# Gate products of the last 128 tokens: float32 against two float32r parts, in a four-layer decoder trunk on one core

## The chip, the core and the metric

The kernel runs on one core of a Trainium2 chip. The metric is the time of one execution on the device in microseconds; several executions are taken and their median is given. One further execution is recorded by the hardware profiler; all rows below come from that one.

Engine names: PE is the matrix engine (PEld its weight loads), DVE the vector engine, ACT the scalar engine, POOL the general one, SP the engine that issues most transfers.

## The reference, cut to what matters

A decoder trunk of four layers works on 256 tokens of 1024 values. Each layer has a token mixer and then `peer`, an expert layer. The change lies in `peer`:

```
def peer(x, w_q, keys, u, v):
    ...
    best, sel = lax.top_k(cand.reshape(n_tok, PEER_HEADS, PEER_TOPK * PEER_TOPK), PEER_TOPK)
    idx = jnp.take_along_axis(cand_idx.reshape(n_tok, PEER_HEADS, -1), sel, axis=-1)
    gate = jax.nn.softmax(best, axis=-1)
    ...
        h = jax.nn.gelu(jnp.einsum('cd,ced->ce', tc, ue).astype(f32), approximate=False)
        return jnp.einsum('ce,ced->cd', gc * h, ve)
```

Each token chooses 8 heads x 16 experts out of 16384, with a softmax gate for each. The kernel does not gather experts. It computes the hidden value of all 16384 experts for all tokens, multiplies it by a dense table of gates that is zero where an expert was not chosen, and multiplies the outcome by all of `v`.

## The kernel before, in words

The work of a layer is written as one stream of 128x1024 weight chunks. `_load` (line 81) has SP fetch a chunk, `_split` (lines 91 and 97) has ACT round it to a float32r high part and DVE subtract that for the low part. `nxt` hands out a chunk and first splits those up to two chunks ahead. A product of float32 quality is then three float32r products: high by high, low by high, high by low (`proj_t`, line 141; `proj_n`, lines 151 to 155).

`peer` has four steps. `peer_scores` makes the routing scores. The first big loop (j from 0 to 127) multiplies chunk j of `u` by the tokens (24 products of 256 columns into a bank `hp`), and ACT writes the Gelu of it to G (line 1051). The second big loop multiplies G, split into parts (lines 1036 and 1037), by the chunks of `v`. Beside the first loop runs the routing: `topk_gen` on DVE, 128 tokens at a time.

The gates get to G in two ways. For the first 128 tokens POOL scatters them into a table in DRAM (`scatter`, line 957), 128 indirect transfers; at j = 124 SP is told to fetch the table piece by piece (`fetch`, line 1022), which waits for the whole scatter, and DVE multiplies G by the pieces (line 1031). For the last 128 tokens `weights_gen` makes the gates on PE, four tokens a unit, 32 units a layer: for each token the product of two one-hot tables, one of the row and one of the column of each chosen expert, the second multiplied by the gate. `topk_gen` ends by transposing row, column and gate into `tab` (line 911).

`weights_gen` is a generator. Each `yield` is a turn, and `pace` gives turns out as the first loop goes on: after the routing is done the rate is 35 turns over the chunks that are left up to 125. In turn u the code before does this:

- `build(u + 1)`: DVE makes both one-hot tables of the next unit by comparing `iota` with `tab` (line 925) and multiplies the column's by the gates (line 927), into a buffer `wk` of two.
- PE: four products (line 941) into the bank `y{u % 4}`.
- `due()`: DVE multiplies the already activated chunks of G by the gates of the unit of two turns ago (line 1006, two pieces).
- `keep` for the last turn's unit: ACT stores its gates where G has not been activated yet (line 999), and a new `due` is kept for the rest.

Chunks that are activated after their gates were stored are taken care of by lines 1054 and 1013: ACT writes the Gelu to a buffer `gtmp` (two of them) and DVE multiplies it into G, one chunk later.

Every engine works in the order in which the code is written: the program is built with a manual schedule for PE, DVE, ACT and SP, and the framework adds the waits between them.

Of the kernel before, what the change touches and what calls it, by code (L numbers as in the profile page):

```python
# [11 lines left out]
F32 = mybir.dt.float32  # L12
F32R = mybir.dt.float32r
# [3 lines left out]
AF = mybir.ActivationFunctionType  # L17
# [27 lines left out]
class Kernel:  # L45
# [744 lines left out]
    def topk_gen(self, ids, val, tab, ready):  # L790


        nc = self.nc
        V = nc.vector
        svs, sis = self.ring(2, 16, 16), self.ring(2, 16, 16, dt=U32)
# [23 lines left out]
        for t in range(2):  # L819
# [9 lines left out]
            f = sif.rearrange("p (h q) k -> p h q k", q=2)  # L829
# [11 lines left out]
            for a, off in enumerate(OFFS):  # L841
                if a in (0, 1, 2, 3, 4, 5, 8):
                    nb = 16 // (a + 1)
                    na = len([1 for c in range(a, 16) if 16 // (c + 1) == nb])
                    o = cand[:, :, off:off + na * nb].rearrange("p h (a b) -> p h a b", b=nb)
# [7 lines left out]
            shape = [128, 4, 16, 16]  # L853
# [54 lines left out]
        p = self.small((128, 4, 128))  # L908
        for q in range(3):
            nc.tensor.transpose(p[:, q, :], stk[:, q, :], self.ident)  # L910
        V.tensor_copy(tab, p[:, 0:3, :])
        yield 0.55

    def weights_gen(self, tab, keep):


        nc = self.nc
        V = nc.vector
        shape = [128, 2, 4, 128]
        units = {}  # L920

        def build(u):
            ts = slice(124 - 4 * u, 128 - 4 * u)
            ab = self.misc.tile(shape, F32, name="wk", bufs=2)
            V.tensor_tensor(ab, self.iota[:, None, None, :].to_broadcast(shape),  # L925
                            tab[:, 0:2, ts][:, :, :, None].to_broadcast(shape), op=OP.is_equal)
            V.tensor_mul(ab[:, 1], ab[:, 1], tab[:, 2, ts][:, :, None].to_broadcast([128, 4, 128]))
            units[u] = ab

        build(0)  # L930
        yield 1
        kept, due = None, None
        for u in range(34):
            if u + 1 < 32:
                build(u + 1)
            p = None
            if u < 32:
                p = self.ps.tile([128, 4, 128], F32, name=f"y{u % 4}", bufs=1)
                ab = units.pop(u)
                for k in range(4):  # L940
                    nc.tensor.matmul(p[:, k, :], ab[:, 0, k, :], ab[:, 1, k, :], start=True, stop=True)  # L941
            if due is not None:
                due()
            due = keep(256 - 4 * u, kept.rearrange("p t j -> p j t")) if kept is not None else None
            kept = p
            yield 1

# [25 lines left out]
    def peer(self, i, turn):  # L973
        nc = self.nc
        self.new_work()
        iv = self.misc.tile([128, 2, 128], F32, name="gt", bufs=2)
        ids, val = iv[:, 0, :].bitcast(I32), iv[:, 1, :]
        tab = self.misc.tile([128, 3, 128], F32, name="tab", bufs=1)
        self.sc = self.carve(2, 16, 128)
        self.sc_ready, self.paced = 0, 0.0  # L980
        sent = []
# [11 lines left out]
        def keep(t0, p):  # L993

            ts = slice(t0, t0 + 4)
            n = [min(max(done[0] - 64 * f, 0), 64) for f in range(2)]
            for f in range(2):
                if n[f] < 64:
                    nc.scalar.activation(G[f][:, n[f]:64, ts], p[:, 64 * f + n[f]:64 * f + 64, :], AF.Copy)
            done[1] = t0  # L1000

            def due():
                for f in range(2):
                    if n[f]:
                        g = G[f][:, 0:n[f], ts]
                        nc.vector.tensor_mul(g, g, p[:, 64 * f:64 * f + n[f], :])
            return due
# [32 lines left out]
        for j in range(128):  # L1040
# [11 lines left out]
            if td < T:  # L1052
                tmp = self.misc.tile([128, T], F32, name="gtmp", bufs=2)
# [27 lines left out]
        for j in range(n):  # L1081
# [12 lines left out]
            if j in (68, 71, 74, 77):  # L1094
                k = (j - 68) // 3
                self.load_norms(i, nc.sync, slice(k, k + 1))
            if j in (80, 83, 86, 89):
                k = (j - 80) // 3
# [234 lines left out]
```

## Time and profile before

| | before |
|---|---|
| median of 3 runs | 3824.62 us (3823.56 to 3825.99) |
| the profiled execution, its own time | 3826.61 us |
| its span from first to last instruction | 3824.8 us |
| PE busy | 3792.5 us, 99% |
| DVE busy | 2826.6 us, 74% |
| ACT busy | 1878.3 us, 49% |
| POOL busy | 1091.9 us, 29% |

Busy time counts an engine's instructions and not its waits. In the lists of groups a row gives the line, engine, operation, names and shape, the count, then busy time in us and the mean ns of one, then the idle time of the engine just before them and what ended it. In a timeline a row gives the start, the length, the engine, the line and what it was, with the idle time before it in brackets. An arrow points to what a thing was made from or what ended a wait.

### The profile page before, as it was taken

How to read it: one execution, taken by the hardware profiler on the slowest of the kernel's cores; microseconds unless marked ns; L12 is line 12 of the kernel's file. 1: busy time of each engine (PE TensorE's matmuls, PEld its weight loads, DVE VectorE, ACT ScalarE, POOL GpSimd, SP SyncE). 2: the span in 40 equal slices, each digit the busy share in tenths (PEclk: the TensorE clock that was granted, in tenths of full speed). 3: DMA queues.
4: the chain of work that ended last, by engine and by line, in shares of the span. 5: the costliest groups of instructions: out<-in, count | busy, mean ns of one | idle time of the engine just before them, and what ended most of it. 6: DMA issues, size and time to landing. Idle time of an engine off the chain costs nothing. (4 is left out here: it accounts for less than half of the span.)

```text
span 3824.8 us, 67261 instructions
## 1 busy us (share of the span) xinstructions
PE 3792.5 (99%) x25652; PEld 3468.1 (91%) x25652; DVE 2826.6 (74%) x5914; ACT 1878.3 (49%) x3400; POOL 1091.9 (29%) x548
## 2 busy tenths in 40 slices
PE   8999999999999999999999999999999999999999
PEld 7999998888998999988887999998888899998887
DVE  7787776676667887766667788776677788776666
ACT  5544444545554544455555444444555554445554
POOL 0158750000000188720000148860000128780000
PEclk9999999999999999999999999999999999999999
DMA  7667777775444577777762567778775456666665
GB/s 236 201 183 180 174 207 239 246 242 163 142 138 147 171 186 178 176 226 240 250 211 99 168 182 180 177 185 246 245 249 164 144 182 179 160 158 215 215 226 176
DMA packets 400996, 735.35 MB, mean 192 GB/s; under 512 B 102608, under 2 KB 240400, under 8 KB 400160
## 3 DMA queue, kind: packets, MB, share of 16 engines
q1 hardware_dynamic: 326688, 730.60, 59.4%
q0 software_dynamic: 73792, 0.38, 5.5%
q8 instruction: 201, 3.29, 0.3%
q14 instruction: 123, 1.01, 0.1%
q10 hardware_dynamic: 192, 0.07, 0.0%
HBM read 696.01 MB, written 34.89 MB: 191 GB/s over the span
## 5 line engine op out<-in xcount | busy, mean ns | idle before, releaser
L97 DVE TENSOR_TENSOR lo<-raw,hi 128x1024 fp32r<-128x1024 f32 x1182 | 1444.2, 1223 | 595.2 <-ACT hi L91 591.9
L91 ACT ACTIVATE hi<-raw 128x1024 fp32r<-128x1024 f32 x1212 | 1271.2, 1050 | 32.9 <-DMA raw<-in_peer_v 21.2
L957 POOL DMA_INDIRECT gates<-gt x512 | 1017.6, 1988 | 485.0 <-DVE G L808 247.7
L141 PE MATMUL hp<-zh,hi 128*128 128x256 f32 x5312 | 764.0, 286 | 1.6 <-ACT zh L242 0.7
L141 PE MATMUL hp<-zh,lo 128*128 128x256 f32 x5312 | 746.4, 283 | 0.0
L141 PE MATMUL hp<-zl,hi 128*128 128x256 f32 x5312 | 746.1, 283 | 0.0
L141 PEld LDWEIGHTS hp<-zh,hi 128*128 128x128 f32 x5312 | 682.7, 192 | 7.6 <-issue 4.5
L141 PEld LDWEIGHTS hp<-zh,lo 128*128 128x128 f32 x5312 | 685.9, 192 | 0.0
L141 PEld LDWEIGHTS hp<-zl,hi 128*128 128x128 f32 x5312 | 685.8, 192 | 0.0
L155 PE MATMUL y<-hi,wk 128*128 128x512 f32 x2004 | 624.9, 393 | 1.5 <-DVE wk L1037 1.3
L153 PE MATMUL y<-lo,wk 128*128 128x512 f32 x2004 | 623.1, 392 | 0.0
L151 PE MATMUL y<-hi,wk 128*128 128x512 f32 x2004 | 621.1, 390 | 0.0
L97 POOL TENSOR_TENSOR lo<-raw,hi 128x1024 fp32r<-128x1024 f32 x30 | 72.7, 2424 | 1871.8 <-ACT hi L91 1871.8
L1051 ACT ACTIVATE G<-hp 128x256 f32<-128x256 f32 (+26 forms) x512 | 182.6, 357 | 836.8 <-PE hp L141 825.9
L1036 ACT ACTIVATE wk<-G 128x256 fp32r<-128x256 f32 x492 | 205.9, 418 | 656.9 <-issue 625.1
L155 PEld LDWEIGHTS y<-hi,wk 128*128 128x128 f32 x2004 | 375.9, 188 | 85.5 <-DVE wk L1037 2.1
L151 PEld LDWEIGHTS y<-hi,wk 128*128 128x128 f32 x2004 | 375.8, 188 | 84.2 <-ACT wk L1113 0.3
L153 PEld LDWEIGHTS y<-lo,wk 128*128 128x128 f32 x2004 | 376.5, 188 | 80.1
L1037 DVE TENSOR_TENSOR wk<-G,wk 128x256 fp32r<-128x256 f32 x492 | 208.8, 424 | 263.3 <-ACT wk L1036 263.2
L427 ACT ACTIVATE G<-hp 128x256 f32<-128x256 f32 x156 | 59.7, 382 | 203.4 <-PE hp L141 195.9
L925 DVE TENSOR_TENSOR wk<-iota,tab 128x1024 f32<-128x1024 f32 x128 | 156.1, 1219 | 0.0
L1031 DVE TENSOR_TENSOR G<-G,gt 128x128 f32<-128x128 f32 x512 | 144.3, 284 | 7.6 <-DMA gt<-gates 7.4
(202 smaller groups left out, 2611.7 us busy)
## 6 DMA issues: line engine op xcount, KB each, us to landing
raw<-in_peer_u SPq DMA_DIRECT2D x512, 512.0 KB
raw<-in_peer_v SPq DMA_DIRECT2D x512, 512.0 KB
raw<-in_dil_w SPq DMA_DIRECT2D x72, 512.0 KB
gates<-zero SPq DMA_DIRECT2D x256, 128.0 KB
raw<-in_peer_wq SPq DMA_DIRECT2D x64, 512.0 KB
gt<-gates SPq DMA_DIRECT2D x256, 128.0 KB
raw<-in_swa_w SPq DMA_DIRECT2D x20, 512.0 KB
G<-in_lnp SPq DMA_DIRECT2D x16, 512.0 KB
```

The source lines that it names most:

```text
L91: nc.scalar.activation(h[:, :w], r[:, :w], AF.Copy)
L97: eng.tensor_sub(lo[:, :w], r[:, :w], h.bitcast(F32)[:, :w])
L141: mm(ps, w[:, k, :], z[:, k0 + k, :], start=(p == 0 and k == 0), stop=(p == 2 and k == nk - 1))
L151: mm(ps[t][b][:, :s.stop - s.start], zh[:, ts], hi[:, s], start=first, stop=False)
L153: mm(ps[t][b][:, :s.stop - s.start], zh[:, ts], lo[:, s], start=False, stop=False)
L155: mm(ps[t][b][:, :s.stop - s.start], zl[:, ts], hi[:, s], start=False, stop=last)
L925: V.tensor_tensor(ab, self.iota[:, None, None, :].to_broadcast(shape), tab[:, 0:2, ts][:, :, :, None].to_broadcast(shape), op=OP.is_equal)
L957: ins = self.nc.gpsimd.indirect_dma_start(self.gates[i], IndirectOffsetOnAxis(ap=ids[:, k:k + 1], axis=0), val[:, k:k + 1], None, compute_ ...
L1031: nc.vector.tensor_mul(g, g, gts[j // 2][:, j % 2, :])
L1036: nc.scalar.activation(gz[:, 0, :], g, AF.Copy)
L1037: nc.vector.tensor_sub(gz[:, 1, :], g, gz.bitcast(F32)[:, 0, :])
L1051: nc.scalar.activation(g[:, 0:td], ps[:, 0:td], AF.Gelu)
```

## The change

The gate products become float32r. `topk_gen` splits the gates in `tab` into a float32r part and the rest. `build` makes the one-hots in float32r; ACT multiplies the column's one-hots by the rest, token by token, into a third table, and DVE then multiplies them in place by the first part. One product of 256 columns per token gives both halves, with two tokens to a bank, so that a unit takes two banks (`y0` and `y1`, or `y2` and `y3`). `add` sums the halves: ACT copies the second to `gtmp` and DVE adds it to the first, bank by bank, both into the first bank. `due()` stands at the head of the turn, ahead of `build`.

```
-        V.tensor_copy(tab, p[:, 0:3, :])
+        V.tensor_copy(tab[:, 0:3], p[:, 0:3, :])
         yield 0.55
+        V.tensor_copy(tab[:, 3].bitcast(F32R), tab[:, 2])
+        yield 0.28
+        V.tensor_sub(tab[:, 2], tab[:, 2], tab[:, 3])
+        yield 0.28
...
         def build(u):
-            ts = slice(124 - 4 * u, 128 - 4 * u)
-            ab = self.misc.tile(shape, F32, name="wk", bufs=2)
-            V.tensor_tensor(ab, self.iota[:, None, None, :].to_broadcast(shape),
+            o = 124 - 4 * u
+            ts = slice(o, o + 4)
+            ab = self.misc.tile([128, 3, 4, 128], F32R, name="wk", bufs=2)
+            ones = ab.bitcast(F32)[:, 1]
+            V.tensor_tensor(ab[:, 0:2], self.iota[:, None, None, :].to_broadcast(shape),
                             tab[:, 0:2, ts][:, :, :, None].to_broadcast(shape), op=OP.is_equal)
-            V.tensor_mul(ab[:, 1], ab[:, 1], tab[:, 2, ts][:, :, None].to_broadcast([128, 4, 128]))
+            for k in range(4):
+                nc.scalar.activation(ab[:, 2, k, :], ones[:, k, :], AF.Copy, scale=tab[:, 2, o + k:o + k + 1])
+            V.tensor_mul(ab[:, 1], ones, tab[:, 3, ts][:, :, None].to_broadcast([128, 4, 128]))
             units[u] = ab
+
+        def add(p):
+
+            for q in range(2):
+                tmp = self.misc.tile([128, 2, 128], F32, name="gtmp", bufs=2)
+                nc.scalar.activation(tmp, p[q][:, :, 1, :], AF.Copy)
+                V.tensor_add(p[0][:, :, q, :], p[q][:, :, 0, :], tmp)
+            return p[0].rearrange("p a b j -> p (a b) j")
...
         for u in range(34):
+            if due is not None:
+                due()
             if u + 1 < 32:
                 build(u + 1)
             p = None
             if u < 32:
-                p = self.ps.tile([128, 4, 128], F32, name=f"y{u % 4}", bufs=1)
+                p = [self.ps.tile([128, 2, 2, 128], F32, name=f"y{2 * (u % 2) + q}", bufs=1) for q in range(2)]
                 ab = units.pop(u)
                 for k in range(4):
-                    nc.tensor.matmul(p[:, k, :], ab[:, 0, k, :], ab[:, 1, k, :], start=True, stop=True)
-            if due is not None:
-                due()
-            due = keep(256 - 4 * u, kept.rearrange("p t j -> p j t")) if kept is not None else None
+                    nc.tensor.matmul(p[k % 2][:, k // 2], ab[:, 0, k, :], ab[:, 1:3, k, :], start=True, stop=True)
+            due = keep(256 - 4 * u, add(kept).rearrange("p t j -> p j t")) if kept is not None else None
             kept = p
             yield 1
```

In the changed kernel lines 925, 927, 941, 999, 1006, 1013, 1051 and 1054 are 932, 936, 960, 1016, 1023, 1030, 1068 and 1071; new are 935 (scaling), 943 (copy) and 944 (sum).

The first place is DVE in the first layer, one turn and the chunk before it. In brackets stand the semaphores that a row waits for, named by engine or transfer queue; G is the table of hidden values, y a unit's bank. Before:

```order
L97 TENSOR_TENSOR lo<-raw,hi 128x1024 [waits DMAHW2_49,PE_49,Activation_49]
L1013 TENSOR_TENSOR G_4147<-G_4147,gtmp 128x56
L925 TENSOR_TENSOR wk<-iota,tab 128x1024 [waits PE_49]
L927 TENSOR_TENSOR wk<-wk,tab 128x512 [waits DVE_49]
L1006 TENSOR_TENSOR G_1740<-G_1740,y_5202 128x64x4
L1006 TENSOR_TENSOR G_4147<-G_4147,y_5202 128x26x4
L97 TENSOR_TENSOR lo<-raw,hi 128x1024 [waits DMAHW3_49,PE_49,Activation_49]
```

and in the changed kernel:

```order
L97 TENSOR_TENSOR lo<-raw,hi 128x1024 [waits DMAHW2_49,PE_49,Activation_49]
L1030 TENSOR_TENSOR G_4149<-G_4149,gtmp 128x44
L1023 TENSOR_TENSOR G_1740<-G_1740,y_5072 128x64x4 [waits DVE_49]
L1023 TENSOR_TENSOR G_4149<-G_4149,y_5072 128x21x4
L932 TENSOR_TENSOR wk<-iota,tab 128x1024 [waits PE_49]
L936 TENSOR_TENSOR wk<-wk,tab 128x512 [waits DVE_49,Activation_49]
L944 TENSOR_TENSOR y_5165<-y_5165,gtmp 128x2x128 [waits Activation_49]
L944 TENSOR_TENSOR y_5165<-y_5166,gtmp 128x2x128 [waits Activation_49]
L97 TENSOR_TENSOR lo<-raw,hi 128x1024 [waits DMAHW4_49,PE_49,Activation_49]
```

The bank release (1006, now 1023) moved ahead of the build, the multiplication (936) now waits for ACT, and two sums that wait for ACT stand ahead of the next low part.

The second place is ACT at the same point: two chunks and a turn. Before:

```order
L91 ACTIVATE hi<-raw 128x1024 [waits DMAHW3_49]
L1051 ACTIVATE G_4147<-hp 128x188 [waits PE_49]
L1054 ACTIVATE gtmp<-hp 128x68 [waits DVE_49,Activation_49]
L999 ACTIVATE G_4147<-y_5494 128x30x4
L91 ACTIVATE hi<-raw 128x1024 [waits DMAHW4_49]
```

and in the changed kernel:

```order
L91 ACTIVATE hi<-raw 128x1024 [waits DMAHW2_49]
L1068 ACTIVATE G_4149<-hp 128x212 [waits PE_49]
L1071 ACTIVATE gtmp<-hp 128x44 [waits DVE_49]
L935 ACTIVATE wk<-wk,tab 128x128 [waits DVE_49]
L935 ACTIVATE wk<-wk,tab 128x128 x3
L943 ACTIVATE gtmp<-y_5165 128x256 [waits Activation_49]
L943 ACTIVATE gtmp<-y_5166 128x256 [waits DVE_49]
L1016 ACTIVATE G_4149<-y_5165 128x41x4 [waits DVE_49]
L91 ACTIVATE hi<-raw 128x1024 [waits DMAHW4_49]
```

Six activations came in between a chunk's Gelu and the next high part; the first of them, the second copy and the storing each wait for DVE.

The third place is PE at a unit (numbers kept, so that the banks can be told apart). Before, and then changed:

```order
L941 MATMUL y1_6079<-wk_5994 128x128 [waits DVE_49]
L941 MATMUL y1_6079<-wk_5994 128x128 x3
L141 MATMUL hp_6094<-zh_1014,hi_6006 128x256 [waits PE_49,Activation_49]
```

```order
L960 MATMUL y0_6790<-wk_6690 128x256 [waits DVE_49,Activation_49]
L960 MATMUL y1_6791<-wk_6690 128x256
L960 MATMUL y0_6790<-wk_6690 128x256
L960 MATMUL y1_6791<-wk_6690 128x256
L141 MATMUL hp_6809<-zh_1014,hi_6710 128x256 [waits PE_49,Activation_49]
```

A unit now fills two banks by turns and is twice as wide.

## Rows read from the trace of the kernel before

**Rows 1.** The page, busy us, share of the span and instructions of each engine.
```profile
PE 3792.5 (99%) x25652; PEld 3468.1 (91%) x25652; DVE 2826.6 (74%) x5914; ACT 1878.3 (49%) x3400; POOL 1091.9 (29%) x548
```
**Rows 2.** Line 941, first layer: ns min/median/max, first and last start.
```profile
L941 PE MATMUL y<-wk x256: 270/275/275, 338.9 to 528.4; 128*128 128x128 f32 x128
```
**Rows 3.** Window of that stretch: us; PE, PEld, DVE, ACT, POOL busy; clock, DMA.
```profile
338.00:531.00 193.00, 193.00 (x1630) 193.00 (x1630) 147.36 (x234) 84.63 (x199) 155.72 (x84) 1.00 0.75 177
```
**Rows 4.** Timeline of the first layer, 503.9 to 514.4 us.
```profile
503.96 1.05 PE L941 MATMUL y<-wk 128*128 128x128 f32 x8
...
505.28 0.69 DVE L927 TENSOR_TENSOR wk<-wk,tab 128x512 f32<-128x512 f32 x1
...
505.81 1.12 PE L141 MATMUL hp<-zh,lo 128*128 128x256 f32 x8
505.89 0.68 DVE L1006 TENSOR_TENSOR G<-G,y 128x256 f32<-128x256 f32 x2
...
506.77 1.12 PE L141 MATMUL hp<-zl,hi 128*128 128x256 f32 x8
...
508.12 0.26 ACT L1054 ACTIVATE gtmp<-hp 128x108 f32<-128x108 f32 x1
508.26 1.06 ACT L91 ACTIVATE hi<-raw 128x1024 fp32r<-128x1024 f32 x1
...
509.35 1.23 DVE L97 TENSOR_TENSOR lo<-raw,hi 128x1024 fp32r<-128x1024 f32 x1 [1.47 <-ACT hi L91]
...
510.61 1.05 PE L941 MATMUL y<-wk 128*128 128x128 f32 x8
...
514.38 1.05 PE L941 MATMUL y<-wk 128*128 128x128 f32 x8
```
**Rows 5.** Groups of DVE, 338 to 531 us.
```profile
L97 DVE TENSOR_TENSOR lo<-raw,hi 128x1024 fp32r<-128x1024 f32 x58 | 70.9, 1222 | 44.4 <-ACT hi L91 44.3
L925 DVE TENSOR_TENSOR wk<-iota,tab 128x1024 f32<-128x1024 f32 x31 | 37.8, 1220 | 0.0
L927 DVE TENSOR_TENSOR wk<-wk,tab 128x512 f32<-128x512 f32 x31 | 21.5, 692 | 1.1
L1006 DVE TENSOR_TENSOR G<-G,y 128x256 f32<-128x256 f32 (+30 forms) x60 | 18.0, 340 | 0.0
L1013 DVE TENSOR_TENSOR G<-G,gtmp 128x4 f32<-128x4 f32 (+29 forms) x54 | 11.6, 216 | 0.0
```
**Rows 6.** Groups of ACT, 338 to 531 us.
```profile
L91 ACT ACTIVATE hi<-raw 128x1024 fp32r<-128x1024 f32 x57 | 60.8, 1066 | 0.0
L1051 ACT ACTIVATE G<-hp 128x256 f32<-128x256 f32 (+30 forms) x57 | 19.1, 335 | 107.2 <-PE hp L141 105.6 <-issue 1.6
L1054 ACT ACTIVATE gtmp<-hp 128x4 f32<-128x4 f32 (+29 forms) x54 | 11.7, 216 | 0.0
L999 ACT ACTIVATE G<-y 128x244 f32<-128x244 f32 (+30 forms) x31 | 9.0, 290 | 0.0
```
**Rows 7.** Groups of the whole span, shapes kept apart.
```profile
L1051 ACT ACTIVATE G<-hp 128x256 f32<-128x256 f32 x268 | 103.0, 384 | 390.3 <-PE hp L141 383.7 <-issue 6.4
...
L1006 DVE TENSOR_TENSOR G<-G,y 128x256 f32<-128x256 f32 x128 | 52.9, 413 | 0.0
...
L284 ACT ACTIVATE gtmp<-ident,lnst 128x128 f32<-128x128 f32 x7 | 2.8, 403 | 1.6 <-DVE lnst L197 1.6
```
**Rows 8.** Third layer: the chain's last scatter, then SP's timeline behind it.
```profile
2561.43 4.91 DMA gates<-gt
...
2562.53 0.33 SPq L81 DMA_DIRECT2D raw<-in_peer_v  x1
2566.41 0.38 SPq L1022 DMA_DIRECT2D gt<-gates  x1
```
**Rows 9.** PE's timeline at the start of the program.
```profile
13.59 1.91 PE L141 MATMUL hp<-zh,lo 128*128 128x256 f32 x8
15.29 1.59 PE L141 MATMUL hp<-zl,hi 128*128 128x256 f32 x8
```

More of the change, by code (lines that the diff above doesn't have):

```diff
@@ L977, in peer @@
         ids, val = iv[:, 0, :].bitcast(I32), iv[:, 1, :]
-        tab = self.misc.tile([128, 3, 128], F32, name="tab", bufs=1)
+        tab = self.misc.tile([128, 4, 128], F32, name="tab", bufs=1)
         self.sc = self.carve(2, 16, 128)
```

## The prediction

> **What bounds the kernel now.** I read the page's table of engines first [rows 1]: PE is busy for 99% of the span, DVE for 74%, ACT for 49%. Busy time is an average over stages, so I then went to the only stage that the change touches, the one in which the gate products run. The row of line 941 [rows 2] puts it in the first layer at 338.9 to 528.4 us: 256 records, eight to each of 32 units. The window over that stretch [rows 3] shows PE busy in every microsecond (193.00 of 193.00) at a granted clock of 1.00, DVE in 147.4 of 193 us, ACT in 84.6. So PE sets the pace there, and neither of its helpers is far ahead: DVE has 46 us to spare per layer.
>
> The timeline of one round [rows 4] shows the pattern. The chunks' products come in groups of eight that start 0.96 us apart (505.81 to 506.77), so a chunk of 24 products takes 2.88 us. From the start of one unit of four gate products to the next it is 6.65 us where two chunks lie between (503.96 to 510.61) and 3.77 where one does (510.61 to 514.38). Both leave 0.89 us for a unit. The pacing hands out 35 shares over the last 63 chunks, five units to nine chunks, so the 31 intervals of a layer are 25 long and 6 short: 25 x 6.65 + 6 x 3.77 = 189 us, as in [rows 2].
>
> The last thing to read is who waits for whom. In this stage DVE's idle time is the 44.4 us before line 97, ended by ACT's high part [rows 5]; lines 925, 927, 1006 and 1013 wait for next to nothing. ACT's long idle time ends with PE's products [rows 6]. That is a pipeline in one direction, PE to ACT to DVE to PE, with two chunks of slack.
>
> **The change, part by part.**
> *The product.* Four float32 products of 128 columns (0.89 us) become four float32r products of 256 columns. The chunks' products have that form and take 0.96 / 8 = 0.12 us each, so a unit costs 0.48. This takes 0.41 us off PE per unit, 0.41 x 128 = 52 us in all, if PE goes on setting the pace. A unit's round of two chunks then needs 5.76 + 0.48 = 6.24 us of PE.
>
> *The table.* One transposed table is split by two more small DVE operations, about 0.5 us a layer, beside PE work in a stage where DVE idles: nothing.
>
> *Building the one-hots.* ACT gets four multiplications of 128x128 by a column of scales. Nearest row: line 284, 128x128 from SBUF with a scale column, 403 ns [rows 7]. They read the one-hots that DVE has just made, and DVE's multiplication behind them overwrites those same one-hots, so DVE has to stand still until ACT has finished all four. Before, nothing stood between lines 925 and 927.
>
> *Summing the halves.* Per unit ACT copies 128x256 out of PSUM twice (as line 1051 in that form, 384 ns) and DVE adds 128x256 twice. Line 1006, 128x256 with one input from PSUM, gives 413 ns [rows 7]; no row has DVE writing PSUM. I take 0.41; the bounds are 0.41 and, for slower writes, the 0.69 us that line 927 takes for twice the elements [rows 5]. Both copies share one buffer, since the other holds the activated chunk that line 1013 has yet to multiply in, and the order shows it: the second copy waits for DVE. So copy, sum, copy, sum run strictly one after another, and the activation that stores the gates waits for the last sum.
>
> *The banks.* A unit now holds two banks, so two units are in flight, not four. The order moves the old unit's last multiplications ahead of the build, because PE's next unit needs their banks. PE therefore waits, at each unit, for DVE to have done everything that stands ahead of these multiplications: the low parts of the chunks, and through them ACT's high parts.
>
> On ACT, the activation of line 999, now 1016, waits for DVE. Queued behind it stands the chunk's high part (line 91), and for that wait DVE's low part, then the bank release, then PE. So the helpers no longer run as a pipeline: within a round ACT waits for DVE three times and DVE for ACT four times.
>
> **The round.** I add it up from start to start. Where an engine runs on without a wait, its next instruction starts 0.08 us (DVE, 505.28 + 0.69 to 505.89) or some 0.10 us (ACT, 508.12 + 0.26 to 508.26) before the recorded end; from one engine to the other it takes 0.03 us (508.26 + 1.06 to 509.35) [rows 4]. Durations are the stage's means [rows 5, 6], else [rows 7].
> - DVE one-hots 1.22 + 0.03 = 1.25
> - ACT four scalings 4 x 0.40 - 3 x 0.10 + 0.03 = 1.33
> - DVE multiplication 0.69 - 0.08 and first sum 0.41 + 0.03: 1.05 (the first copy fits in beside the multiplication)
> - ACT second copy 0.38 + 0.03 = 0.41; DVE second sum 0.44
> - ACT storing 0.29 - 0.10 = 0.19
> - ACT high part 0.97, activations 0.24 and 0.12, second high part 1.07 + 0.03: 2.43 (DVE's first low part lies beside it)
> - DVE second low part 1.14, line 1013 0.14, two bank releases 0.52: 1.80, and then the next one-hots
>
> Sum 8.90 us, against PE's 6.24: **PE no longer sets the pace**. With one chunk between units the 2.43 falls to 1.10: 7.57. A layer's 31 intervals take 25 x 8.90 + 6 x 7.57 = 268 us. The first round has no sums, storing or release yet (2.0 less) and the second no release (0.5 less): 265.5, against 189, so 76.5 us more in each layer, 306 in all. The profiled execution took 3826.61 us, 1.8 over its span and 2.0 over the median of the three runs; 3827 + 306 = 4133, and against the median the same rise gives 4131. I say **4132**.
>
> Bounds. If the scale column cost nothing, a scaling would be no slower than line 999's mean of 0.29 [rows 6]: 4 x 0.11 less, 55 us over 124 rounds, 4077. I keep 0.40, since line 284 is the same operation on the same shape. If DVE's writes to PSUM take 0.69, twice 0.28 more: 69 us, 4201. Six crossings a round at 0.03 could be twice that where an instruction waits for two engines: 22 us more.
>
> Two rules of the Trainium skill. The rows above show PE at 100% and the helpers at 76% and 44%. The page Perfetto Trace Analysis, section Identifying the Most-Contended Engine, says to optimize the engine with the highest occupancy first; by it this change gains, and the rival A below is what it would give. The same page, section Matmuls under Optimizing Tensor Performance, says that independent groups should rotate through PSUM banks so that evacuating one overlaps the next; this speaks against the step from four units in flight to two, and no run so far shows its price.
>
> **Rivals.**
> *A: PE still sets the pace, so it gets faster.* This is so if the round of ACT and DVE stays below 6.24 us, that is if 2.66 us of it overlap: the scalings (1.33) and the two sums with their second copy (1.3) would just do. For it: DVE's total, 147.4 us plus 64 sums of 0.33 a layer, is 168 in the 180 us that would remain. Against it: the waits of DVE on ACT are in the program, and both engines work in order. Its price is 52 us at best, 3774. But in the third layer the fetch of the gates already waits for the last scatter (it lands at 2561.43 + 4.91 = 2566.34; the queue, free at 2562.86, issues at 2566.41) [rows 8], and POOL's pace doesn't come from PE, so that layer would keep little of its 13 us. If every layer kept as little as the 3.5 us by which that fetch could be late without stopping PE, the gain would be 14: 3813. **Chance 5%**, one of it within 0.2%.
>
> *B: the clock falls.* PE would stand still for 2.66 us of each round of 8.9. At the very start of the program, a few microseconds after PE's first inputs, groups of eight such products started 1.70 us apart (13.59, 15.29) instead of 0.96 [rows 9]: the lower level, 1.2 GHz. The Trainium skill, page TensorE: Matmul & The Clock Gate, section What's actually happening, has the gate throttled by default and released by activity; the start agrees. If the whole stage ran so, nine chunks and five units would take 27 x 1.70 + 5 x 0.85 = 50 us of PE, against 4 x 8.90 + 7.57 = 43.2: 7 us more a cycle, 6.2 cycles a layer, 170 us in all, 4300. But PE would then work without a pause, which speaks for the clock coming back. **Chance 10%**, most of it part of the way.
>
> *C: the float32r product costs more than 0.12 us.* It may cost up to the 0.89 it replaces; PE then needs 6.65 a round and still waits. It changes nothing in my sum.
>
> **How the numbers follow.** Forecast 85%, A 5%, B 10%. The range 4060 to 4230 takes in the bounds of the scalings (4077) and of the sums with slow crossings (4223), and a small part of B. No change that is less than 0.2% (8 us) can be told from none here; faster by more has 0.04, within it 0.01, slower 0.95.
>
> **What would show it.** PE busy in about 70% of the stage, waiting in each unit for DVE's bank release; a stage of some 265 us a layer from first to last gate product; DVE idle before line 936 for 1.3 us and ACT before 935, 943 and 1016. In the rest of the program nothing moves. The forecast is wrong if intervals between units stay near 6.2 us (A), if the granted clock falls there (B), or if a round's parts don't add, say because the four scalings take far from 1.3 us.

## The result and the profile after

| | before | after |
|---|---|---|
| median of four runs, us | 3824.92 (3823.56 to 3825.99) | 4141.81 (4140.70 to 4143.04) |
| profiled execution: span, us | 3824.8 | 4141.0 |

The ratio is 1.0829, 95% interval 1.0815 to 1.0842: 316.9 us slower. Forecast were 4132 and a rise of 306.

The page of the changed kernel, engines and the shares of the chain that ended last (followed back from the last instruction, at each step to what released it or to the one before it on its engine):

```profile
PE 3853.3 (93%) x25140; PEld 3506.6 (85%) x25140; DVE 2934.0 (71%) x6178; ACT 2123.4 (51%) x4168; POOL 1029.2 (25%) x548
...
PE 71%; DVE 16%; ACT 9%; issue 3%; DMA 1%; SPq 0%; ACTq 0%; DVEq 0%
```

Against [rows 1] only ACT's share has risen, by two points, and PE's has fallen from 99% to 93%. The chain tells more: DVE and ACT hold a quarter of it.

Line 960 (941 before) in the first layer, with what ended PE's idle time before it (us, times); then the window of that stretch, its columns as in [rows 3]:

```profile
L960 PE MATMUL y<-wk x128: 274/282/553, 340.8 to 607.9; 128*128 128x256 f32 x128
...
  DVE G L1023: 62.6, 29
```
```profile
341.00:608.00 267.00, 203.78 (x1472) 198.57 (x1472) 171.26 (x294) 142.40 (x383) 144.54 (x85) 0.90 0.53 125
```

The stage takes 267.1 us instead of 189.5 [rows 2], in the other layers 267.0, 266.1 and 266.5. PE, busy without a gap in [rows 3], is now busy for 76% of it (about 70% was forecast); of the 63.2 us in which it is idle, the bank release (line 1023, before 1006) ends 62.6. The granted clock has a mean of 0.90.

The timeline of one round, from one one-hot build to the next (start, us; in brackets the idle time before, and what ended it):

```profile
502.09 1.22 DVE L932 TENSOR_TENSOR wk<-iota,tab 128x1024 fp32r<-128x1024 f32 x1
...
502.32 1.19 PE L960 MATMUL y<-wk 128*128 128x256 f32 x4 [2.49 <-DVE G L1023]
...
503.35 1.28 ACT L935 ACTIVATE wk<-wk,tab 128x128 fp32r<-128x128 f32 x4 [2.77 <-DVE wk L932]
504.54 0.36 ACT L943 ACTIVATE gtmp<-y 128x256 f32<-128x256 f32 x1
504.66 0.69 DVE L936 TENSOR_TENSOR wk<-wk,tab 128x512 fp32r<-128x512 f32 x1 [1.35 <-ACT wk L935]
...
505.27 0.42 DVE L944 TENSOR_TENSOR y<-y,gtmp 128x256 f32<-128x256 f32 x1
505.73 0.39 ACT L943 ACTIVATE gtmp<-y 128x256 f32<-128x256 f32 x1 [0.83 <-DVE y L944]
...
506.15 0.43 DVE L944 TENSOR_TENSOR y<-y,gtmp 128x256 f32<-128x256 f32 x1 [0.45 <-ACT gtmp L943]
506.61 0.27 ACT L1016 ACTIVATE G<-y 128x116 f32<-128x116 f32 x1 [0.50 <-DVE y L944]
506.78 1.05 ACT L91 ACTIVATE hi<-raw 128x1024 fp32r<-128x1024 f32 x1
...
509.15 1.21 DVE L97 TENSOR_TENSOR lo<-raw,hi 128x1024 fp32r<-128x1024 f32 x1
...
510.44 0.62 DVE L1023 TENSOR_TENSOR G<-G,y 128x256 f32<-128x256 f32 x2
510.98 1.21 DVE L932 TENSOR_TENSOR wk<-iota,tab 128x1024 fp32r<-128x1024 f32 x1
```

From 502.09 to 510.98 it is 8.89 us. From the one-hots to the storing (502.09 to 506.78), while one of the two helpers works, the other mostly stands in front of it: in the rows shown each bracket of ACT names DVE, and each of DVE names ACT. In [rows 5, 6] lines 925, 927 and 1006 waited for next to nothing, and only line 97 waited for ACT.

The waits of the same stretch, first layer (us in total, times, longest):

```profile
ACT wk L935 <- DVE wk L932: 68.4, 31, 2.9
PE y L960 <- DVE G L1023: 62.6, 29, 4.1
...
DVE wk L936 <- ACT wk L935: 41.8, 31, 1.4
DVE lo L97 <- ACT hi L91: 36.7, 31, 1.4
...
ACT gtmp L943 <- DVE y L944: 24.7, 30, 0.8
```

### The profile page after: what moved, and what is told of

Same layout as the page of the kernel before. It is cut to its first block, busy times and chain, and to the rows that moved or that the text cites. A ratio compares the mean times of both kernels' runs of the same rounds, so it can differ in the third digit from the quotient of the medians.

```text
span 4141.0 us, 67273 instructions
## 1 busy us (share of the span) xinstructions
PE 3853.3 (93%) x25140; PEld 3506.6 (85%) x25140; DVE 2934.0 (71%) x6178; ACT 2123.4 (51%) x4168; POOL 1029.2 (25%) x548
## 4 chain that ended last, share of the span: by engine, by line
PE 71%; DVE 16%; ACT 9%; issue 3%; DMA 1%; SPq 0%; ACTq 0%; DVEq 0%
PE hp L141 30%; PE y L151 12%; PE y L155 12%; PE y L153 12%; DVE lo L97 5%; ACT wk L935 3%; ACT hi L91 3%; DVE wk L932 3%; DVE y L944 2%; DVE wk L936 2%; DVE G L1023 2%; ACT gtmp L943 1%; DVE G L1030 1%; ACT G L1016 1%; PE sm L777 1%
## 5 line engine op out<-in xcount | busy, mean ns | idle before, releaser
L974 POOL DMA_INDIRECT gates<-gt x512 | 954.9, 1865 | 485.1 <-DVE G L809 247.7
L141 PE MATMUL hp<-zh,hi 128*128 128x256 f32 x5312 | 794.5, 295 | 1.8 <-ACT zh L242 1.0
L141 PE MATMUL hp<-zh,lo 128*128 128x256 f32 x5312 | 774.4, 290 | 0.0
L141 PEld LDWEIGHTS hp<-zh,hi 128*128 128x128 f32 x5312 | 723.2, 202 | 7.7 <-issue 4.5
L141 PEld LDWEIGHTS hp<-zh,lo 128*128 128x128 f32 x5312 | 717.3, 200 | 0.0
L1068 ACT ACTIVATE G<-hp 128x256 f32<-128x256 f32 (+26 forms) x512 | 181.9, 355 | 460.3 <-PE hp L141 460.2
L960 PE MATMUL y<-wk 128*128 128x256 f32 x512 | 107.2, 340 | 253.6 <-DVE G L1023 249.0
L960 PEld LDWEIGHTS y<-wk 128*128 128x128 f32 x512 | 81.1, 221 | 275.3 <-issue 223.2
L935 ACT ACTIVATE wk<-wk,tab 128x128 fp32r<-128x128 f32 x512 | 163.9, 390 | 277.7 <-DVE wk L932 277.7
```

Of the source, the lines that this page charges most:

```text
L141: mm(ps, w[:, k, :], z[:, k0 + k, :], start=(p == 0 and k == 0), stop=(p == 2 and k == nk - 1))
L935: nc.scalar.activation(ab[:, 2, k, :], ones[:, k, :], AF.Copy, scale=tab[:, 2, o + k:o + k + 1])
L960: nc.tensor.matmul(p[k % 2][:, k // 2], ab[:, 0, k, :], ab[:, 1:3, k, :], start=True, stop=True)
L974: ins = self.nc.gpsimd.indirect_dma_start(self.gates[i], IndirectOffsetOnAxis(ap=ids[:, k:k + 1], axis=0), val[:, k:k + 1], None, compute_ ...
L1068: nc.scalar.activation(g[:, 0:td], ps[:, 0:td], AF.Gelu)
```

## The experiments

The theory is the prediction's: the stage's length is the serial sum of hand-offs between ACT and DVE, closed by the bank release. The runs of before taken beside each group of four had medians of 3826.68 and 3826.16 us.

### The scalings' roles swapped
Against the changed kernel:
```
+ V.tensor_mul(ab[:, 2], ones, tab[:, 3, ts]...)
  for k in range(4):
-     activation(ab[:, 2, k, :], ones[:, k, :], Copy, scale=tab[:, 2, ...])
+     activation(ab[:, 1, k, :], ones[:, k, :], Copy, scale=tab[:, 2, ...])
- V.tensor_mul(ab[:, 1], ones, tab[:, 3, ts]...)
```


> The roles of the scalings are swapped: DVE writes the second part's table itself, right behind the one-hots and without a wait, and ACT scales the first part in place. The amount of work on both engines stays, and DVE no longer stands before its multiplication. Theory (the round is the serial sum of hand-offs between ACT and DVE, closed by the bank release): the four scalings (1.3 us) now stand between DVE's multiplication and the first copy, and the copy, which lay beside the multiplication, comes behind them. Rounds of 9.3 us instead of 8.9, some 4190 us, 50 slower than the changed kernel. Rival (what is lost is DVE's idle time ahead of its multiplication, 172.6 us in 128 waits): that wait is gone, so about 170 us less than 4142, near 3970.

By the edit DVE still multiplies by the float32r part and ACT by the rest; what they exchange is the table that each writes. DVE writes the third one and needs no wait, ACT works in place (line 934 is DVE's multiplication here, 936 ACT's scalings).

Measured: 4193.69 us, ratio to before 1.0960 (1.0928 to 1.0992), 4 us above the time expected; most rounds with two chunks took 9.2 to 9.4. Its waits over the whole span:

```profile
ACT wk L936 <- DVE wk L934: 343.4, 115, 3.6
...
DVE y L944 <- ACT gtmp L943: 243.6, 239, 1.7
```

DVE's wait before its multiplication is gone, and the program is 52 us longer. The idle time of DVE has moved to the sums: line 944 now waits 243.6 us for ACT, against 56.5 in the changed kernel. The idle time in front of one line was not the price; the chain was.

### Both scalings on DVE
```
- for k in range(4):
-     activation(ab[:, 2, k, :], ones[:, k, :], Copy, scale=tab[:, 2, ...])
+ V.tensor_mul(ab[:, 2], ones, tab[:, 2, ts]...)
```


> DVE does the second part's scaling too, with one multiplication of 128x512 (0.69 us, 0.61 to the next start), instead of ACT's four. Theory (serial sum of hand-offs): 1.33 us of the round and one crossing there and back are replaced by 0.61 on the same engine, 0.55 to 0.7 us less in each round of 8.9: 4055 to 4075 us, rounds near 8.4. Rival (DVE, at 71% the busier helper, is the bound by its amount of work): 128 x 0.61 = 78 us more, near 4220. Second rival (ACT's scalings cost nothing, the lowered clock does): no change, 4142.

Measured: 4077.81 us, 1.0657 (1.0626 to 1.0688). DVE, the busier helper, does 0.6 us more in each round, and the program is 64 us shorter, since one instruction on the same engine replaces four and two crossings. Rounds with two chunks took 8.2 to 8.4 us at the full granted clock, some 0.6 less than in the changed kernel, as the theory has it; those at a clock of about 0.80 took 8.4 to 8.75, and four at about 0.70 9.35 to 9.6. The total is 3 us above the range expected.

### Without the sums
```
- due = keep(256 - 4 * u, add(kept)...)
+ due = keep(256 - 4 * u, kept[0]...)
```


> The two copies and two sums are left out, so the stored gates are the first bank as it is (the sum of the halves is left out of the computation). Scalings, float32r products of 256 columns, two banks per unit and the release at the head of the turn stay. Theory (serial sum): the round loses first sum, second copy, second sum and the storing's wait, some 1.3 to 2 us of 8.9, and comes near PE's own 6.24: rounds of 6.9 to 7.3, about 3890 to 3920 us. Rival (two units in flight, not the sums, make PE wait): rounds stay above 8 and the time above 4050. Rival (the sums' durations alone, 2 x 0.4 on DVE): 4142 - 128 x 0.8 = 4040.

Measured: 3923.00 us, 1.0253 (1.0223 to 1.0282), 3 us above the range; rounds with two chunks of 6.9 to 7.2. The two copies and sums cost 219 us of the 317. On DVE alone the 256 sums of the changed kernel last 0.43 us each, 110 in all: half of what leaving them out gives back. PE's wait for the release, first layer:

```profile
PE y L960 <- DVE G L1023: 20.6, 18, 2.0
```

Eight of the program's 124 rounds ran at a granted clock of 0.80 and took 8.4 to 8.6 us, 1.5 more than the others: 12 us, more than what the time lies above the range. One of them and its neighbour (columns as in [rows 3]; the clock is the third from the end):

```profile
366.84:375.26 8.42, 7.95 (x52) 7.77 (x53) 4.87 (x9) 4.29 (x11) 7.51 (x4) 0.80 0.66 140
375.26:382.20 6.94, 6.45 (x53) 6.28 (x53) 4.90 (x9) 4.32 (x12) 5.72 (x5) 1.00 0.63 146
```

### Two units in flight, alone
Against the kernel before:
```
+ if due is not None: due()      # at the head of the turn
- p = self.ps.tile([128, 4, 128], F32, name=f"y{u % 4}", bufs=1)
+ p = self.ps.tile([128, 4, 128], F32, name=f"y{u % 2}", bufs=1)
- if due is not None: due()      # behind the products
```


> The kernel before with one thing of the change alone: two units in flight instead of four, and the bank release at the head of the turn. Products stay float32 of 128 columns, nothing is scaled or summed on ACT. Theory: the bank wait alone makes PE wait for DVE's low parts once in each unit, but the helpers' round without sums is shorter than PE's 6.65, so only part of it shows: rounds of 7 to 7.6, 3870 to 3910 us. Rival (two units in flight are the whole price): above 4050. Rival (they cost nothing as long as the helpers' own round is under 6.65): 3825.

Measured: 3906.92 us, 1.0211 (1.0181 to 1.0240); rounds of 7.2 to 7.7 where 6.65 stood [rows 4]. One release and the unit behind it:

```profile
513.40 0.68 DVE L1006 TENSOR_TENSOR G<-G,y 128x256 f32<-128x256 f32 x2
...
514.22 1.13 PE L943 MATMUL y<-wk 128*128 128x128 f32 x8 [0.72 <-ACT G L1051]
```

The bracket names ACT's line 1051, but that one had ended at 513.83; the release ends at 514.08, and PE starts 0.14 us later, as it does in the changed kernel (510.44 + 0.62 to 511.20). The bank wait has a price of its own, 80 us, without any new work on ACT or DVE. This run changes the number of banks and the place of the release together; the run with the early release, below, has two units in flight as well, and there PE waits for no bank. The rule cited in the prediction, that groups should rotate through the banks (the Trainium skill, page Perfetto Trace Analysis, section Matmuls), agrees with this run.

### Product and banks, neither scaling nor sums
Against the changed kernel, the four scalings and the two copies and sums left out, and ab[:, 0:2] as the product's second operand.

> The float32r products of 256 columns, two banks a unit and the release at the head of the turn, without any scaling by the second part and without the two copies and sums (the product's second half is computed from other columns and never read, so the second part is left out of the computation). Theory: the bank wait is left as in the run with two units in flight, the unit is 0.41 us shorter, so rounds of two chunks near 6.9 to 7.2 and of one chunk near 3.8, 3850 to 3870 us. Rival (the 256-column product is the gain that was meant, and the bank wait shows only together with the scalings): 52 us less than before, near 3775 to 3812.

Measured: 3858.47 us, 1.0084 (1.0063 to 1.0104). Against the run before it this is 48 us less: the cheaper product is worth about what the prediction gave it (52), and the bank wait alone more than eats it up. The time lies in the range expected.

### The same with an early release
```
- due = keep(256 - 4 * u, kept[0]...)
+ keep(256 - 4 * u, kept[0]...)()
```


> As the run before it, but the old unit's last multiplications follow right behind its storing instead of waiting for the next turn (the second part is left out of the computation here too). The banks then come free a whole round earlier, and PE sets the pace: rounds of 6.26 us against 6.65, as much as 50 us less by PE alone, 3774. Theory of the rival A: the fetch of the gates waits for the last scatter, whose pace does not come from PE; with what the four layers' fetches have in hand (5.0, 6.9, 0.05 and 6.9 us) no more than about 19 us can come out, so 3805 to 3812, and the rest turns up as PE waiting for the first rows of the next stage. Rival (no such limit): 3774.

Measured: 3782.52 us, 0.9888 (0.9871 to 0.9904). Line 956 (the gate products here) in the first layer, then PE's waits over the span (lines 1050 and 1051 split G into parts, as 1036 and 1037 before):

```profile
L956 PE MATMUL y<-wk x128: 274/278/283, 339.5 to 515.0; 128*128 128x256 f32 x128
```
```profile
PE y L155 <- DVE wk L1051: 6.3, 3, 2.3
...
PE y L151 <- ACT wk L1050: 3.1, 2, 2.8
```

The stage takes 175.5 us, 14.0 less than before, with rounds of 6.21: 56 in four layers, of which 43.6 arrive in the time. A limit of 19 us, as I expected it, isn't there. Part of it shows: PE waits 9.4 us (6.3 + 3.1) for the factors of the products at lines 151 and 155, which come after the fetch; the kernel before has 1.3 in the first of these rows. But the scatters came faster too. One of them took a mean of 1937 ns here and 1988 before, and the third layer's 128 starts lie within 304.6 us instead of 315.9. What sets their pace was not tried.

### The same work in another order
Against the changed kernel:
```
  def build(u):
      ...                        # one-hots only
+     self.pend.append(scale)    # 4 scalings and the multiplication
  def add(p):
+     p, ab = p                  # the old unit's one-hot buffer
+     tmp = ab[:, 0]...
+     for q in range(2): activation(tmp[:, q], p[q][:, :, 1, :], Copy)
      for q in range(2):
-         activation(tmp, p[q][:, :, 1, :], Copy)
          V.tensor_add(p[0][:, :, q, :], p[q][:, :, 0, :], tmp...)
  for u in range(34):
+     flush()
-     if due is not None: due()
+     if kept is not None: sums now; storing and release to pend
      build(u + 1)
-     the unit's products
+     the unit's products to pend
  # in the loop over the chunks, once per chunk:
+ self.flush()
```


> The whole computation of the changed kernel in another order: the copies go to the old unit's own one-hot buffer and not to the shared one, so both copies and both sums run back to back; the four scalings and the multiplication come one chunk after the one-hots, and the storing and the bank release follow one chunk after the sums, so that no instruction at the head of a queue waits for the engine that has just been started; the products are issued behind a chunk. If the round of hand-offs is the price, and not the amount of work, the same work then fits beside PE's 6.24 us: rounds of 6.3 to 6.7, 36 us less than before by the engines alone, and with the scatters' limit about 3805 to 3815. Rival (the added work on ACT and DVE, 0.8 and 1.6 us a unit, is itself the price): above 3900.

Measured: 3798.57 us, 0.9925 (0.9908 to 0.9941): 27.6 us faster than the kernel before and 343 faster than the changed one, with the whole computation. Its timeline, one round (952 is the copies here, 954 the sums, 975 the products, 1032 the storing, 938 the scalings):

```profile
492.03 0.66 ACT L952 ACTIVATE wk<-y 128x256 fp32r<-128x256 f32 x2
...
493.17 0.99 DVE L954 TENSOR_TENSOR y<-y,wk 128x256 f32<-128x256 f32 x2
...
493.91 0.63 PE L975 MATMUL y<-wk 128*128 128x256 f32 x4
...
494.20 0.22 ACT L1032 ACTIVATE G<-y 128x64 f32<-128x64 f32 x1 [0.55 <-DVE y L954]
...
494.20 1.23 DVE L932 TENSOR_TENSOR wk<-iota,tab 128x1024 fp32r<-128x1024 f32 x1
495.34 1.22 DVE L97 TENSOR_TENSOR lo<-raw,hi 128x1024 fp32r<-128x1024 f32 x1
...
495.52 1.28 ACT L938 ACTIVATE wk<-wk,tab 128x128 fp32r<-128x128 f32 x4 [1.10 <-DVE wk L932]
...
500.15 0.63 PE L975 MATMUL y<-wk 128*128 128x256 f32 x4
```

From 493.91 to 500.15 it is 6.24 us, exactly PE's own work as the prediction added it up. The same copies, sums, scalings and release are all there; DVE fills the scalings' time with a chunk's low part (495.34), and both sums run back to back. The stage takes 181.9 us in the first layer, 6.4 more than with the early release, since from the second single chunk on the round with it takes 3.6 to 4.1 (3.33 there) and the one behind it 6.8 (6.21). The time is 6 us below the range expected: the four stages are 30.7 us shorter than before, 27.6 of that arrive, and the limit by the scatters hardly shows. Four things were moved together (copies, scalings, release, products); which of them would do alone was not tried.

### Every gate product four times
```
- for k in range(4):
+ for k in 4 * (0, 1, 2, 3):
      matmul(p[k % 2][:, k // 2], ab[:, 0, k, :], ab[:, 1:3, k, :], ...)
```


> The changed kernel with every gate product issued four times over into the same banks (the same result, 1.44 us more of PE's work in each unit, in time in which it waits). Theory (PE's lowered clock in the stage costs nearly nothing, as PE waits there anyway): the time stays within 12 us of 4142, while the granted clock in the stage rises, since PE stands still for 1.2 us of each round and no longer for 2.7. Rival (the short stretches at half the clock lengthen rounds): with the clock back the time falls by 15 us or more. Rival (PE's own work is on the round): 124 x 1.44 us more, 4320.

Measured: 4167.47 us, 1.0891 (1.0869 to 1.0913), 25.7 above the changed kernel. That is neither the theory's 12 us nor what either rival gives. Two neighbouring rounds, each from one unit's first product to the next (columns as in [rows 3]; the clock is the third from the end):

```profile
504.76:514.80 10.04, 9.39 (x65) 9.22 (x65) 5.89 (x11) 4.98 (x13) 8.52 (x6) 0.83 0.53 118
514.80:523.68 8.88, 7.88 (x64) 7.71 (x65) 5.81 (x11) 4.87 (x13) 7.36 (x6) 1.00 0.52 94
```

The second, at full clock, lasts 8.88 us, as in the changed kernel, although PE has 1.44 us more to do: PE's own work is not on the round. The first, at a granted clock of 0.83, lasts 10.04. The stage's mean clock rose to 0.96 or 0.97, but the lower level did not go away: five or six two-chunk rounds of each layer, 21 in all, took 9.85 to 10.2 us, some 1.15 more than their neighbours. That is 24 us, nearly the whole difference. So the lowered clock can have a price, which the expectation had left out; the last section says where it comes from.

## Why the prediction was right

**The round.** Term by term, forecast and the timeline above:

| from start to start | forecast | measured |
|---|---|---|
| one-hots to scalings (502.09 to 503.35) | 1.25 | 1.26 |
| four scalings (to 504.66) | 1.33 | 1.31 |
| multiplication, first sum (to 505.73) | 1.05 | 1.07 |
| second copy (to 506.15) | 0.41 | 0.42 |
| second sum (to 506.61) | 0.44 | 0.46 |
| storing (to 506.78) | 0.19 | 0.17 |
| high parts and activations (to 509.15) | 2.43 | 2.37 |
| low part to next one-hots (to 510.98) | 1.80 | 1.83 |
| sum | 8.90 | 8.89 |

No work of PE stands in this sum, and the run with every product four times over bears that out. One term came out right by another path than the one forecast: the row at 509.15 has no bracket, so DVE's first low part and line 1030 (507.86 to 509.15) filled the time of ACT's second high part, which ended at 509.11. As far as the rows show, it is chance that the two end together.

Rounds with one chunk took 7.5 to 7.6 (7.57), those with two 8.8 to 9.0, but for five of 9.4 to 9.5 at a lower clock. The first round was 6.3 (6.9 forecast), the second 9.6 to 9.7 (8.4), so that step, two small subtractions, was wrong for both. The second unit's products follow PE's other products without a wait, so that the first round is nearly PE's own (6.21 in the run with the early release), and the time by which the helpers are behind falls on the second. The two errors point opposite ways and together miss by 0.7, which is luck.

**The stage.** 265.5 was forecast, 266.1 to 267.1 measured. The four stages rose by 309 us instead of 306. Some 8 us of the rise lie outside them, which I had put at nothing: the first unit of the first layer starts at 340.8 and not 338.9, with four scalings ahead of its multiplication now, and the stretches between the stages are 1 to 2.5 us longer. What makes those longer stays open. So "in the rest of the program nothing moves" did not hold, by 8 of 317 us.

**The durations.** One scaling took 390 ns (403 taken from [rows 7]), one sum 429 (410 taken): line 944 writes PSUM and is hardly slower than line 1023, which writes SBUF (413). The upper bound of 0.69 was far off.

**The parts.** By the runs: two units in flight with the release at the head of the turn cost 80 us (3906.9 against 3826.7), the product gives back 48, the scalings add 65 (3923.0 against 3858.5; 12 of it at a lower clock), copies and sums 219. These steps lead from one kernel to the other, so their sum, 315, must be the whole difference (4141.8 against 3826.7) and proves nothing; another order of steps would share it out differently.

**Rival A** fell because the 2.66 us do not overlap in this order. In another they do: 3798.6. Its best case, 3774, lies 8.5 us below the run with the early release; its limit by the scatters, 3813, was too strict. **Rival B** came true in part: the clock does fall in the stage, to a mean of 0.90, which the prediction had named as a sign that it would be wrong. The time did not follow: in the changed kernel that costs some 3 us (last section). The forecast took the clock as full and still had the rise right, because no work of PE is in the sum. **C** changed nothing, as said.

## What to carry to other kernels

Before moving work onto engines with idle time, write down one round from start to start, on each engine in program order, and add up what waits for what. Two helpers at 71% and 51% were the bound because they took turns; the wait with the most of DVE's idle time in the stage (line 936) was not where the time went. Where a round is a chain, try to give each hand-off a chunk's distance (issue the consumer one chunk later) before taking work away: here such an order turned the same work from 317 us slower into 28 us faster.

## What the runs showed of the hardware

**The granted clock inside the stage.** Before, it was 1.00 [rows 3]. Three rounds of the changed kernel, each from one unit's first product to the next:

```profile
502.32:511.20 8.88, 7.71 (x52) 7.54 (x53) 5.80 (x11) 4.87 (x13) 7.36 (x6) 0.84 0.50 98
511.20:520.10 8.90, 6.47 (x53) 6.29 (x53) 5.83 (x11) 4.82 (x13) 7.68 (x5) 1.00 0.60 127
...
458.63:468.14 9.51, 8.92 (x53) 8.74 (x53) 5.81 (x11) 5.01 (x13) 7.99 (x6) 0.71 0.60 124
```

PE had waited 2.49 us ahead of the first of them, and its products then ran at the lower level, 1.2 GHz, for part of the round. PE is busy for 7.71 us instead of 6.47, but the round is no longer than its neighbour: the lost time comes out of PE's waiting. Such rounds are about half of them. In the first layer the mean clock of 15 of the 31 rounds was 0.71 to 0.92, and PE had waited 2.3 to 4.1 us ahead of each; the 13 rounds behind a shorter wait (1.2 at most) kept 0.99 or more. Three rounds behind a wait of 2.4 to 3.3 us kept 0.98 or more as well; why, I can't explain from these rows.

Only where the clock fell to 0.71 or 0.73 in a round with two chunks did the round grow, to 9.4 or 9.5; there are five such rounds in the program, and they cost some 3 us. What such a round costs is read from ACT's activation of the unit's first chunk (line 1068), behind which the next high part stands in ACT's queue. Its row in the round at 458.63 of the changed kernel, in the slow round of the run with every product four times, and in the slow round and its neighbour of the run without the sums:

```profile
464.71 0.34 ACT L1068 ACTIVATE G<-hp 128x200 f32<-128x200 f32 x1 [0.55 <-PE hp L141]
```
```profile
511.31 0.32 ACT L1068 ACTIVATE G<-hp 128x180 f32<-128x180 f32 x1 [1.05 <-PE hp L141]
```
```profile
371.95 0.37 ACT L1068 ACTIVATE G<-hp 128x240 f32<-128x240 f32 x1 [1.63 <-PE hp L141]
...
378.87 0.37 ACT L1068 ACTIVATE G<-hp 128x236 f32<-128x236 f32 x1
```

These rounds are 0.6, 1.15 and 1.5 us longer than their neighbours, about what ACT waits there for the late products. In the round at 502.32 this row (507.73, 0.31 us) has no wait, and the round did not grow.

That activity releases the throttle (the Trainium skill, page TensorE: Matmul & The Clock Gate, section What's actually happening) agrees with the stage's mean in the first layer: 0.90 in the changed kernel, 0.96 with the products issued four times, 1.00 with the early release, where PE never waits for a gate product.

**The pace of the scatters isn't fixed.** One took a mean of 1988 ns before, 1937 with the early release and 1865 in the changed kernel. I had taken their pace as fixed. The changed kernel's stage moved 125 GB/s instead of 177, but that is not the reason by itself: with the early release the stage moved 189 GB/s, more than before, and the scatters were faster all the same. What sets their pace stays open.
